# Raw activations for block 1's input projection, the last MLP column by token chunk, and a wide final power in a hybrid conv and state-space layer

## The chip, the cores and the metric

The kernel runs on one core of a Trainium2 chip. The metric is the device time of one execution in microseconds. The core has five engines with queues of their own, which run their instructions in order and wait for each other by semaphores: TensorE (PE, matrix products; PEld is its weight load), VectorE (DVE), ScalarE (ACT), GpSimd (POOL) and SyncE (SP, here the issuer of most transfers). DMA queues move data between HBM and the on-chip memory (SBUF); products land in PSUM.

## The reference

One decoder layer over 2064 tokens (16 meta tokens and 2048 others) with 1024 features:

```python
hn = rms_norm(h, norm_mix_g)
proj = hn @ w_in                          # b_gate, c_gate, v, u: 512 columns each
conv_out = b_gate * causal_dwconv(c_gate * v, conv_w)
ssm_out = s5_group_ssm(u, ...)            # scan over tokens, GELU, half-GLU
mixed = concat([rms_norm(conv_out), rms_norm(ssm_out)])
h = h + mixed @ w_out
hn = rms_norm(h, norm_ffn_g)
up = causal_dwconv(hn @ w_up, ffn_conv_w, ffn_conv_b)   # 2 x 2816 columns, width 3
h = h + (silu(up[..., :2816]) * up[..., 2816:]) @ w_down
y = rms_norm(h, norm_final_g)[:, 16:]
```

`rms_norm` divides each token's vector by its root mean square, so the factor 1/rms is one number for each token; the gain is one number for each feature. Everything is in float32.

## The kernel before

Features lie on the 128 partitions, tokens on the free axis. The tokens are cut into three blocks b = 0, 1, 2 of 688, each into two chunks (quarters q = 2b and 2b+1 of 344 tokens; in block 0 the MLP has 672, two times 336). A float32 product is made of three products of halves: `parts` makes hi (a rounded copy, ScalarE, L248) and lo (the rest, VectorE, L109), and `product` issues hi·hi (L138), hi·lo (L139) and lo·hi (L142).

**Input projection.** `u_block(b)` makes the 512 columns u for the state-space part in four products `pu`, each written from PSUM to `ut` and sent to HBM; `conv_block(b)` makes for j = 0 to 3 the three products `cv`, `cc`, `cb` and from them the convolution: vs from cv, `cvt` = cc·vs, three taps into `tc`, and tc·cb. These products share a PSUM pool of three buffers. The program writes u_block(0), conv_block(0), u_block(2), u_block(1), conv_block(1), conv_block(2), and the steps of the state-space part and the preparation of the next x are put between the products from queues (`prep`, `ssm`). Engines keep the order that a scheduler makes of the program.

x of a quarter can be prepared in two ways. `prep_x` loads it, takes 1/rms of its tokens (`inv_rms`) and splits x·gain·(1/rms): four multiplies t_c (L241) and one hi and one lo instruction for each half of the features. `raw_x` splits x·gain alone, four hi (L393) and four lo (L394) instructions for each half, and takes 1/rms beside it into `rs_of[b]`; since 1/rms is one factor for each token, it is then multiplied in behind the products. Before the change block 0's x and the x for u_block(2) are made by `raw_x`, and all others by `prep_x`. A third argument, `late`, puts the split of a quarter into a list that a later product takes.

`inv_rms_of` has a chain over four engines: the squares summed over features, six small products `st` (L188) with ones so that the sums stand on 115 partitions by 3 columns, mean and epsilon `sv` (VectorE, L198), the power −0.5 `sr` (GpSimd, L199), three diagonals `dg` (L203), one product `sb` (L208) that spreads them to 128 partitions by 344 tokens, and a copy `rs` (ScalarE, L213).

**MLP.** The up projection of one f (128 gate and 128 value columns) goes by seven products of a two-by-two scheme (b11, t4, t1, t2, b22, b21, t3) into z_0 and z_1 (gate and value, both chunks of tokens). `activate` then makes the convolution (ScalarE L1449, two multiply-adds on VectorE L115), silu, the product of gate and value, and its parts `ah`, `al`. 22 f go in chunks of 4, 4, 4, 3, 3 and 4, and after each chunk `down` adds its part of the down projection: `dn` products over the chunk's f, added to HBM by GpSimd's DMA. The products over a pair of output tiles take the last f of the chunk at the end. Under the last chunk of block b the next block's operands (v_b, h_t, l_t and others of `prep_mlp`) are made. The last chunk of block 2 goes by token chunks c, its rows stay in SBUF (`acc`), their squares are summed into `tail_sum` and `tq`, and `finish_last` takes the final 1/rms and multiplies the eight rows.

Of the kernel before, what the change touches and what calls it, by code (L numbers as in the profile page):

```python
# [11 lines left out]
F32 = mybir.dt.float32  # L12
# [5 lines left out]
P = 128  # L18
# [39 lines left out]
def layer_kernel(ctx, tc, xq, pk, w_in, w_glu, w_out, w_up, w_down, ssm_s, ssm_m, y):  # L58
# [317 lines left out]
    rs_of = {}  # L376

    def raw_x(q, res, b, other=False, late=None):
# [30 lines left out]
        yield from inv_rms(xs, QL, f"c{q}", rs_of[b][:, q % 2, :])  # L409

# [479 lines left out]
    def u_block(b, hs, last=False):  # L890
        rhs = rhs_of(hs)
        for m in range(4):
            if last and m == 3:
                while len(late) < 2:
                    prep.step()
            ps = unit(rhs, f"pu_{b}_{m}", m == 0 or last and m == 3)
            ut = cvp.tile([P, NJ, 86], F32, tag="ut", bufs=2, name=f"ut_{b}_{m}")
            if last and m == 3:
                take_late(2)
            by_j = lambda a: a.rearrange("p c (x j) -> p c x j", j=NJ)  # L900
            out = ut.rearrange("p j (c x) -> p c x j", c=2)
            if b in rs_of:
                mul(out, by_j(ps[:, :, :QL]), by_j(rs_of[b]))
            else:
                S.activation(out, by_j(ps[:, :, :QL]), AF.Copy)
            dma(out=u_d[:, m, :, b * 86 : b * 86 + 86].rearrange("j p c -> p j c"), in_=ut)
            after_unit(n_prep=5 if last else 1)

    def conv_block(b, hs, late_after=False, n_prep=1):
        rhs = rhs_of(hs)  # L910

        for j in range(4):
            pv_ = unit(rhs, f"cv_{b}_{j}", False)
            vs = cvp.tile([P, B2], F32, tag="cs", bufs=3, name=f"vs_{b}_{j}")
            if b == 0:
                mul(two(vs), pv_[:, :, :QL], rs_of[0])
# [6 lines left out]
            if b == 0:  # L923
                mul(two(vs), two(vs), rs_of[0])
# [6 lines left out]
            if b == 0:  # L931
                mul(two(tp), two(tp), rs_of[0])
# [69 lines left out]
    prep.add(prep_x(2, hc[1]), prep_x(3, hc[1], other=True, late=late))  # L1002
# [408 lines left out]
    def finish_last(rows, c, terms):  # L1411

        s0, n = y_at(2, c)
        rs = yield from inv_rms_of(terms, D, n, f"last{c}", keep=True)
        for m0, m1 in ((0, 1), (1, 2), (2, 4), (4, 6), (6, 8)):
            for m in range(m0, m1):
                mul(rows(m, c), rows(m, c), rs)
# [13 lines left out]
    for b in range(3):  # L1431
# [16 lines left out]
        def conv(z, t, a):  # L1448
            S.activation(a, z[:, nz - no :], AF.Identity, scale=tap(2, t), bias=col(C_FB + t))  # L1449
# [4 lines left out]
            axpy(a, z[:, nz - no - 1 : nz - 1], tap(1, t), a)  # L1454
            axpy(a, z[:, nz - no - 2 : nz - 2], tap(0, t), a)
# [18 lines left out]
        def up(f, end=False):  # L1474
# [27 lines left out]
            later.append(activate(f, (g, v)))  # L1502
# [3 lines left out]
            tt(v2, X.unsqueeze(1).to_broadcast([P, 2, n]), v2, ALU.add)  # L1506
# [9 lines left out]
        def down(ci, ms, cs=(0, 1), into=None):  # L1516
# [16 lines left out]
            for ks in (range(nk - 1), range(nk - 1, nk)) if len(ms) > 1 else (range(nk),):  # L1533
                for m, ps, w in todo:
# [154 lines left out]
```

## Time and profile before

| | |
|---|---|
| three timed runs | 2183.53, 2181.94, 2178.26 us |
| median | 2181.94 us |
| the profiled execution's own time | 2178.72 us |
| its span in the trace | 2177.0 us |
| mean granted TensorE clock | 0.987 |
| PE busy | 2112.7 us, 97% |
| VectorE, ScalarE, GpSimd busy | 1671.2, 1089.1 and 153.6 us |

The trace holds one execution. Its span leaves 1.7 us of the execution's time outside. A timeline row has the start, the duration, the engine, the line of the kernel, the operation, output and inputs by name, the shape, and in brackets the idle time of that engine before it and what ended it; a row with xN stands for N instructions in a row.

### The profile page before, as it was taken

Reading aid. Unit: us, or ns where it says so; the run is one execution under the profiler, and the core shown is the slowest. Engines: PE = TensorE matmul, PEld = TensorE weight load, DVE = VectorE, ACT = ScalarE, POOL = GpSimd, SP = SyncE. Lnnn points to the kernel's source line nnn. Section 1 sums busy time; section 2 is a strip of 40 time slices with the busy share of each in tenths; the row PEclk is TensorE's granted clock in tenths of the full one; section 3 lists DMA queues with packets and bytes.
Section 4 is the critical chain, followed back from the end, with each engine's and each line's share of the span. In section 5 each row is a group of like instructions: output and inputs, shape, how many; then the busy total and the mean of one; then the engine's idle time right before and its main releaser. Section 6 shows DMA issues by size and latency. Waiting matters only on the chain. (4 is left out here: it accounts for less than half of the span.)

```text
span 2177.0 us, 33169 instructions
## 1 busy us (share of the span) xinstructions
PE 2112.7 (97%) x13012; PEld 2053.0 (94%) x13012; DVE 1671.2 (77%) x2539; ACT 1089.1 (50%) x1659; POOL 153.6 (7%) x174
## 2 busy tenths in 40 slices
PE   8998999999899999999999999999999999999997
PEld 7997999999899999999999999999999999999996
DVE  8788498866857887786669878777868968757776
ACT  4144334236423465555556556555556546545555
POOL 0000000000000000100111010110011010010000
PEclk9898999999999999999999999999999999999998
DMA  7377544352566245725554363744555272564463
GB/s 236 108 210 192 147 142 146 118 162 84 185 223 200 83 109 134 185 70 122 128 135 107 110 157 92 186 111 142 129 131 130 89 191 77 142 133 101 93 173 107
DMA packets 170750, 300.29 MB, mean 138 GB/s; under 512 B 32416, under 2 KB 104800, under 8 KB 170464
## 3 DMA queue, kind: packets, MB, share of 16 engines
q1 hardware_dynamic: 149856, 246.41, 36.8%
q0 software_dynamic: 19584, 47.52, 13.1%
q10 hardware_dynamic: 1152, 4.23, 0.5%
q8 instruction: 102, 1.67, 0.3%
q14 instruction: 56, 0.46, 0.1%
HBM read 214.29 MB, written 83.82 MB: 137 GB/s over the span
## 5 line engine op out<-in xcount | busy, mean ns | idle before, releaser
L109 DVE TENSOR_TENSOR wl_up<-wr_up,wh_up 128x1024 fp32r<-128x1024 f32 x198 | 242.0, 1222 | 137.6 <-ACT wh_up L248 134.9
L138 PE MATMUL dn<-ah,wh_dn 128*128 128x344 f32 (+1 forms) x1024 | 327.7, 324 | 10.2 <-ACT ah L248 8.9
L139 PE MATMUL dn<-al,wh_dn 128*128 128x344 f32 (+1 forms) x1024 | 326.0, 321 | 0.2
L248 ACT ACTIVATE wh_up<-wr_up 128x1024 fp32r<-128x1024 f32 x198 | 210.0, 1061 | 226.8 <-PE dn L139 59.8
L1444 PE MATMUL xy<-h_t,wh_up 128*128 128x344 f32 (+1 forms) x792 | 262.3, 331 | 0.8 <-DVE z L109 0.8
L1446 PE MATMUL xy<-h_t,wl_up 128*128 128x344 f32 (+1 forms) x792 | 252.9, 319 | 0.0
L1445 PE MATMUL xy<-l_t,wh_up 128*128 128x344 f32 (+1 forms) x792 | 252.3, 319 | 0.0
L142 PE MATMUL dn<-ah,wl_dn 128*128 128x344 f32 (+1 forms) x1024 | 248.6, 321 | 0.0
L138 PEld LDWEIGHTS dn<-ah,wh_dn 128*128 128x128 f32 x1024 | 193.7, 190 | 14.6 <-ACT ah L248 9.7
L1546 POOL DMA_DIRECT2D h_d<-ev x136 | 118.3, 870 | 1256.0 <-ACT ev L1542 1242.5
L139 PEld LDWEIGHTS dn<-al,wh_dn 128*128 128x128 f32 x1024 | 194.9, 190 | 2.0 <-DVE al L109 1.2
L1444 PE MATMUL xy<-h_b,wh_up 128*128 128x344 f32 (+1 forms) x528 | 175.2, 333 | 4.7 <-ACT ev L1542 1.9
L142 PEld LDWEIGHTS dn<-ah,wl_dn 128*128 128x128 f32 x1024 | 178.6, 190 | 0.0
L1445 PE MATMUL xy<-l_b,wh_up 128*128 128x344 f32 (+1 forms) x528 | 168.5, 319 | 0.0
L1446 PE MATMUL xy<-h_b,wl_up 128*128 128x344 f32 (+1 forms) x528 | 167.1, 319 | 0.0
L1444 PEld LDWEIGHTS xy<-h_t,wh_up 128*128 128x128 f32 x792 | 148.9, 188 | 18.3 <-ACT z L1489 11.4
L248 ACT ACTIVATE wh_dn<-wr_dn 128x512 fp32r<-128x512 f32 (+1 forms) x144 | 85.7, 595 | 134.7 <-issue 56.3
L1445 PEld LDWEIGHTS xy<-l_t,wh_up 128*128 128x128 f32 x792 | 149.5, 189 | 0.0
L1446 PEld LDWEIGHTS xy<-h_t,wl_up 128*128 128x128 f32 x792 | 149.3, 188 | 0.0
L115 DVE SCALAR_TENSOR_TENSOR g<-z,pv,g 128x688 f32<-128x688 f32 (+1 forms) x132 | 122.3, 927 | 24.0 <-ACT g L1449 23.2
L115 DVE SCALAR_TENSOR_TENSOR v<-z,pneg,v 128x688 f32<-128x688 f32 (+1 forms) x132 | 122.5, 928 | 10.3 <-ACT v L1449 9.0
L109 DVE TENSOR_TENSOR wl_dn<-wr_dn,wh_dn 128x512 fp32r<-128x512 f32 (+1 forms) x144 | 92.4, 645 | 46.0 <-ACT wh_dn L248 45.2
(413 smaller groups left out, 5326.2 us busy)
## 6 DMA issues: line engine op xcount, KB each, us to landing
wr_up<-in_w_up SPq DMA_DIRECT2D x132, 512.0 KB, 5.5
h_d<-ev POOLq DMA_DIRECT2D x88, 344.0 KB, 6.8
wr_dn<-in_w_down SPq DMA_DIRECT2D x96, 256.0 KB, 2.6
wr_cw<-in_w_in SPq DMA_DIRECT2D x36, 512.0 KB, 4.5
h_d<-ev POOLq DMA_DIRECT2D x48, 336.0 KB, 6.8
x_c<-in_xq SPq DMA_DIRECT2D x16, 688.0 KB, 4.6
wr_dn<-in_w_down SPq DMA_DIRECT2D x48, 192.0 KB, 2.3
xr<-in_xq SPq DMA_DIRECT2D x24, 344.0 KB, 3.8
```

Source lines behind the costliest of these rows:

```text
L109: V.tensor_tensor(out, a, b, op=op)
L115: V.scalar_tensor_tensor(out=out, in0=a, scalar=s, in1=b, op0=ALU.mult, op1=ALU.add)
L138: T.matmul(ps[c], hi[:, k, :], xh, start=k == 0, stop=False)
L139: T.matmul(ps[c], hi[:, k, :], xl, start=False, stop=False)
L142: T.matmul(ps[c], lo[:, k, :], xh, start=False, stop=k == nk - 1)
L248: S.activation(hi, t, AF.Copy)
L1444: T.matmul(ps, hi[:, j, :], xh[:, j, :], start=start and j == 0, stop=False, **kw)
L1445: T.matmul(ps, hi[:, j, :], xl[:, j, :], start=False, stop=False, **kw)
L1446: T.matmul(ps, lo[:, j, :], xh[:, j, :], start=False, stop=j == 3, **kw)
L1546: G.dma_start(out=h_d[:, m, s0 : s0 + no], in_=ev, accum_op=ALU.add)
```

## The change

The diff has three parts, in three places of the program.

**A. Block 1's x.** Quarters 2 and 3 go by `raw_x`. So `u_block(1)` reads PSUM with a VectorE multiply by `rs_of[1]` and not with a ScalarE copy, after both quarters' 1/rms are there (`rs_done`), and `conv_block(1)` has the three multiplies for each j that `conv_block(0)` has: vs from PSUM times rs (in place of a ScalarE copy), vs times rs again, tc times rs.

**B. The last f of the last chunk of every block.** `activate_halves` goes through the convolution, silu, product and split by token chunk; the value's last addition is in two halves; and the first pair of `down` tiles of the last chunk takes its last f chunk by chunk. The copies of the halo (`context`) now stand ahead of the first tap in all `activate`s.

**C. The end.** For the last token chunk `finish_last` sums squares with a 128-wide matrix of ones, two products of 344 columns, so that every partition has every token's sum; mean and epsilon (128x344) on VectorE, the power (128x344) on GpSimd, no diagonal and no broadcast; rows 3 and 6 of the eight are multiplied on GpSimd, the others on VectorE.

```diff
--- before.py
+++ after.py
@@ -373,7 +373,7 @@
     def rs_tile(name):
         return cp.tile([P, 2, QM], F32, tag="rsk", bufs=1, name=name)
 
-    rs_of = {}
+    rs_of, rs_done = {}, {}
 
     def raw_x(q, res, b, other=False, late=None):
 
@@ -407,6 +407,7 @@
         if b not in rs_of:
             rs_of[b] = rs_tile(f"rs_{b}")[:, :, :QL]
         yield from inv_rms(xs, QL, f"c{q}", rs_of[b][:, q % 2, :])
+        rs_done[b] = rs_done.get(b, 0) + 1
 
 
     sgn = col(C_SGN)
@@ -900,6 +901,8 @@
             by_j = lambda a: a.rearrange("p c (x j) -> p c x j", j=NJ)
             out = ut.rearrange("p j (c x) -> p c x j", c=2)
             if b in rs_of:
+                while rs_done.get(b, 0) < 2:
+                    prep.step()
                 mul(out, by_j(ps[:, :, :QL]), by_j(rs_of[b]))
             else:
                 S.activation(out, by_j(ps[:, :, :QL]), AF.Copy)
@@ -912,24 +915,24 @@
         for j in range(4):
             pv_ = unit(rhs, f"cv_{b}_{j}", False)
             vs = cvp.tile([P, B2], F32, tag="cs", bufs=3, name=f"vs_{b}_{j}")
-            if b == 0:
-                mul(two(vs), pv_[:, :, :QL], rs_of[0])
+            if b < 2:
+                mul(two(vs), pv_[:, :, :QL], rs_of[b])
             else:
                 S.activation(two(vs), pv_[:, :, :QL], AF.Copy)
             after_unit(n_prep=n_prep)
             pc = unit(rhs, f"cc_{b}_{j}", False)
             cv = cvp.tile([P, B2 + 2], F32, tag="cvt", bufs=1, name=f"cvt_{b}_{j}")
             V.tensor_copy(cv[:, 0:2], halo[:, j, :])
-            if b == 0:
-                mul(two(vs), two(vs), rs_of[0])
+            if b < 2:
+                mul(two(vs), two(vs), rs_of[b])
             tt(two(cv[:, 2:]), pc[:, :, :QL], two(vs), ALU.mult)
             V.tensor_copy(halo[:, j, :], cv[:, B2 : B2 + 2])
             tp = cvp.tile([P, B2], F32, tag="cs", bufs=3, name=f"tc_{b}_{j}")
             S.activation(tp, cv[:, 2:], AF.Copy, scale=col(C_CW + 8 + j))
             axpy(tp, cv[:, 1 : B2 + 1], col(C_CW + 4 + j), tp)
             axpy(tp, cv[:, 0:B2], col(C_CW + j), tp)
-            if b == 0:
-                mul(two(tp), two(tp), rs_of[0])
+            if b < 2:
+                mul(two(tp), two(tp), rs_of[b])
             after_unit(n_prep=n_prep)
             if late_after and j == 3:
                 while len(late) < 2:
@@ -999,7 +1002,7 @@
     next(ahead[0])
     conv_block(0, hc[0], late_after=True, n_prep=4)
 
-    prep.add(prep_x(2, hc[1]), prep_x(3, hc[1], other=True, late=late))
+    prep.add(raw_x(2, hc[1], 1), raw_x(3, hc[1], 1, other=True, late=late))
     u_block(2, hu, last=True)
     until(hc[1], 2)
     prep.add(prep_x(4, hc[2]), prep_x(5, hc[2], late=late))
@@ -1411,10 +1414,20 @@
     def finish_last(rows, c, terms):
 
         s0, n = y_at(2, c)
-        rs = yield from inv_rms_of(terms, D, n, f"last{c}", keep=True)
+        if c == 0:
+            rs = yield from inv_rms_of(terms, D, n, f"last{c}", keep=True)
+        else:
+
+            ps = aux_tile("st_last")[:, :n]
+            for i, a in enumerate(terms):
+                T.matmul(ps, ones, a, start=i == 0, stop=i == len(terms) - 1)
+            v, rs = z_tile("v_last")[:, :n], z_tile("r_last")[:, :n]
+            V.tensor_scalar(v, ps, 1.0 / D, EPS, op0=ALU.mult, op1=ALU.add)
+            G.tensor_tensor(rs, v, mhalf[:, 0:1].to_broadcast([P, n]), op=ALU.pow)
         for m0, m1 in ((0, 1), (1, 2), (2, 4), (4, 6), (6, 8)):
             for m in range(m0, m1):
-                mul(rows(m, c), rows(m, c), rs)
+                eng = G if c and m in (3, 6) else V
+                eng.tensor_tensor(rows(m, c), rows(m, c), rs, op=ALU.mult)
             for m in range(m0, m1, 2):
                 mm = min(2, m1 - m)
                 a = acc[m // 2].rearrange("p (m c) t -> p c m t", c=2)[:, c, m % 2 : m % 2 + mm, :n]
@@ -1445,14 +1458,42 @@
                 T.matmul(ps, hi[:, j, :], xl[:, j, :], start=False, stop=False, **kw)
                 T.matmul(ps, lo[:, j, :], xh[:, j, :], start=False, stop=j == 3, **kw)
 
-        def conv(z, t, a):
-            S.activation(a, z[:, nz - no :], AF.Identity, scale=tap(2, t), bias=col(C_FB + t))
+        def context(z, t):
+
             if b:
                 S.activation(z[:, :o], halo[:, t, :], AF.Copy)
             if b < 2:
                 S.activation(halo[:, t, :], z[:, nz - 2 :], AF.Copy)
-            axpy(a, z[:, nz - no - 1 : nz - 1], tap(1, t), a)
-            axpy(a, z[:, nz - no - 2 : nz - 2], tap(0, t), a)
+
+        def conv_of(z, t, a, i, n):
+
+            i0 = nz - no + i
+            a = a[:, i : i + n]
+            S.activation(a, z[:, i0 : i0 + n], AF.Identity, scale=tap(2, t), bias=col(C_FB + t))
+            axpy(a, z[:, i0 - 1 : i0 - 1 + n], tap(1, t), a)
+            axpy(a, z[:, i0 - 2 : i0 - 2 + n], tap(0, t), a)
+
+        def conv(z, t, a):
+            context(z, t)
+            conv_of(z, t, a, 0, no)
+
+        def activate_halves(f, zs):
+
+            v, g = (fp.tile([P, MAX_OUT], F32, tag="g", bufs=3, name=f"{c}_{b}_{f}")[:, :no] for c in "vg")
+            hi, lo = (fp.tile([P, MAX_OUT], F32R, tag="act", bufs=10, name=f"a{c}_{b}_{f}")[:, :no] for c in "hl")
+            context(zs[0], f)
+            for c in range(2):
+                conv_of(zs[0], f, g, c * nn, nn)
+                h = g[:, c * nn : (c + 1) * nn]
+                S.activation(h, h, AF.Silu)
+            yield
+            context(zs[1], FT + f)
+            act[f] = (hi, lo)
+            for c in range(2):
+                conv_of(zs[1], FT + f, v, c * nn, nn)
+                r = slice(c * nn, (c + 1) * nn)
+                mul(v[:, r], g[:, r], v[:, r])
+                parts(v[:, r], hi[:, r], lo[:, r])
 
         def activate(f, zs):
 
@@ -1499,11 +1540,15 @@
             form(z1, w, 1, "b21")
             tt(g2[:, 0, :], z1, g2[:, 0, :], ALU.add)
             work()
-            later.append(activate(f, (g, v)))
+            later.append((activate_halves if end else activate)(f, (g, v)))
             form(X, w, 0, "t3", start=False)
             if end:
                 work()
-            tt(v2, X.unsqueeze(1).to_broadcast([P, 2, n]), v2, ALU.add)
+            if end:
+                for c in range(2):
+                    tt(v2[:, c, :], X, v2[:, c, :], ALU.add)
+            else:
+                tt(v2, X.unsqueeze(1).to_broadcast([P, 2, n]), v2, ALU.add)
             feed.done()
             mark[0] = g[:, o : o + 1]
             if f < f0_last:
@@ -1531,6 +1576,11 @@
                 return tuple(a[:, cs[i] * nn : (cs[i] + 1) * nn] for a in act[f0 + k])
 
             for ks in (range(nk - 1), range(nk - 1, nk)) if len(ms) > 1 else (range(nk),):
+                if len(ms) > 1 and ks[0] == nk - 1 and ci == last:
+                    for i in range(len(cs)):
+                        for m, ps, w in todo:
+                            product([ps[i]], w, lambda k, _: rhs_down(k, i), nk, ks=ks)
+                    continue
                 for m, ps, w in todo:
                     product(ps, w, rhs_down, nk, ks=ks)
             for m, ps, _ in todo:
```

How the instructions move at the three places follows as the engines' queues have them, the numbers at the end of names being serial numbers of tiles. First VectorE ahead of u_block(1): before, from the last squares of the second quarter (sq_c) to its split;

```order
L109 TENSOR_TENSOR sq_c_0_2030<-sq_c_0_2030,sq_c_1_2032 128x4x344
L109 TENSOR_TENSOR ut_3_2118<-pu_3_2063,rs_1437 128x86x8
L109 TENSOR_TENSOR sq_c_0_2030<-sq_c_0_2030 128x2x344
L109 TENSOR_TENSOR wl_u_2193<-wr_u_1977,wh_u_2192 128x1024
L109 TENSOR_TENSOR sq_c_0_2030<-sq_c_0_2030 128x344
L198 TENSOR_SCALAR sv_c_2041<-st_c_2037 115x3
L203 TENSOR_SCALAR dg_c_2045<-ident,sr_c_2042 115x115 x3
L241 SCALAR_TENSOR_TENSOR t_c_0_2053<-x_c_0_1968,pv,rs_c_2051 128x344 x4
L241 SCALAR_TENSOR_TENSOR t_c_1_2058<-x_c_1_1970,pv,rs_c_2051 128x344 x4
L109 TENSOR_TENSOR l_c_0_2120<-t_c_0_2053,h_c_0_2119 128x4x344
```

and now:

```order
L109 TENSOR_TENSOR sq_c_0_2032<-sq_c_0_2032 128x344
L394 SCALAR_TENSOR_TENSOR l_c_0_2096<-x_c_0_1970,pv,h_c_0_2095 128x344 x4
L394 SCALAR_TENSOR_TENSOR l_c_1_2106<-x_c_0_2030,pv,h_c_1_2105 128x344 x4
L109 TENSOR_TENSOR ut_3_2094<-pu_3_2039,rs_1437 128x86x8
L198 TENSOR_SCALAR sv_c_2121<-st_c_2117 115x3
L109 TENSOR_TENSOR wl_u_2196<-wr_u_1977,wh_u_2195 128x1024
L203 TENSOR_SCALAR dg_c_2125<-ident,sr_c_2122 115x115 x2
L109 TENSOR_TENSOR wi_2585<-tab_coarse,tab_fine 128x544
L203 TENSOR_SCALAR dg_c_2125<-ident,sr_c_2122 115x115
```

The t_c and the wide l_c are gone, the split by lo (L394, from x and hi alone) stands ahead of sv_c, and sv_c and the diagonals dg_c stand behind eight l_c, ut and a weight's lo part. On PE, in the same place, before:

```order
L139 MATMUL pu_2_2249<-l_c_0_1956,wh_u_2130 128x344
L188 MATMUL st_c_2037<-ones,sq_c_0_2030 115x1 x3
L208 MATMUL sb_c_2049<-dg_c_2045,ones 128x344
L138 MATMUL pu_0_2129<-h_c_0_2119,wh_u_1973 128x344
L138 MATMUL pu_1_2191<-h_c_0_2119,wh_u_2064 128x344
L138 MATMUL pu_2_2249<-h_c_0_2119,wh_u_2130 128x344
```

and now:

```order
L142 MATMUL pu_3_2039<-h_c_1_1795,wl_u_1899 128x344
L188 MATMUL st_c_2117<-ones,sq_c_0_2032 115x1 x3
L138 MATMUL pu_0_2132<-h_c_0_1869,wh_u_1973 128x344
L139 MATMUL pu_0_2132<-l_c_0_1870,wh_u_1973 128x344
L142 MATMUL pu_0_2132<-h_c_1_1879,wl_u_1974 128x344
L208 MATMUL sb_c_2129<-dg_c_2125,ones 128x344
L138 MATMUL pu_0_2132<-h_c_0_2095,wh_u_1973 128x344
```

Before, u_block(1) had products of its first quarter (h_c_0_1955 and others) ahead of st and sb and those of the second behind them; now pu_0 has its 24 products of the first quarter between st and sb (rows 4 and 5 are the first and the last shown), and those of the second quarter behind sb.

Second, VectorE at the last f (21) of block 1, before:

```order
L115 SCALAR_TENSOR_TENSOR g_21_15985<-z_21_0_15853,pv,g_21_15985 128x688
L109 TENSOR_TENSOR wl_dn_5_3_15994<-wr_dn_5_3_15888,wh_dn_5_3_15993 128x512
L115 SCALAR_TENSOR_TENSOR v_21_15984<-z_21_1_15854,pneg,v_21_15984 128x688
L109 TENSOR_TENSOR l_t_2_16119<-v_b_2_15390,h_t_2_16118 128x4x344
L115 SCALAR_TENSOR_TENSOR v_21_15984<-z_21_1_15854,pneg,v_21_15984 128x688
L1190 SCALAR_TENSOR_TENSOR v_b_2_15390<-v_b_2_15390,v_b_2_15392 128x4x344
L109 TENSOR_TENSOR v_21_15984<-g_21_15985,v_21_15984 128x688
L109 TENSOR_TENSOR l_t_2_16279<-v_b_2_15391,h_t_2_16278 128x4x344
```

and now:

```order
L115 SCALAR_TENSOR_TENSOR g_21_16007<-z_21_0_15875,pv,g_21_16007 128x344 x4
L109 TENSOR_TENSOR z_21_1_15876<-xy_21_15877,z_21_1_15876 128x344 x2
L109 TENSOR_TENSOR wl_dn_5_3_16023<-wr_dn_5_3_15910,wh_dn_5_3_16022 128x512
L115 SCALAR_TENSOR_TENSOR v_21_16006<-z_21_1_15876,pneg,v_21_16006 128x344 x4
L109 TENSOR_TENSOR v_21_16006<-g_21_16007,v_21_16006 128x344 x2
L1193 SCALAR_TENSOR_TENSOR v_b_2_15412<-v_b_2_15412,v_b_2_15414 128x4x344
L109 TENSOR_TENSOR al_21_16009<-v_21_16006,ah_21_16008 128x344 x2
```

The multiply v<-g,v stood behind l_t and a step of v_b, and now its halves stand ahead of v_b, as do the last taps. Third, VectorE behind the last product of the program, before:

```order
L109 TENSOR_TENSOR acc_20684<-dn_5_7_1_21050,acc_20684 128x344
L198 TENSOR_SCALAR sv_last_21074<-st_last_21067 115x3
L203 TENSOR_SCALAR dg_last_21078<-ident,sr_last_21075 115x115 x3
L109 TENSOR_TENSOR acc_20675<-acc_20675,sb_last_21082 128x344 x2
L109 TENSOR_TENSOR acc_20678<-acc_20678,sb_last_21082 128x344 x2
L109 TENSOR_TENSOR acc_20681<-acc_20681,sb_last_21082 128x344 x2
L109 TENSOR_TENSOR acc_20684<-acc_20684,sb_last_21082 128x344 x2
```

now, with GpSimd's last rows behind VectorE's:

```order
L109 TENSOR_TENSOR acc_20728<-dn_5_7_1_21094,acc_20728 128x344
L1425 TENSOR_SCALAR v_last<-st_last 128x344
L1430 TENSOR_TENSOR acc_20719<-acc_20719,r_last 128x344 x2
L1430 TENSOR_TENSOR acc_20722<-acc_20722,r_last 128x344
L1430 TENSOR_TENSOR acc_20725<-acc_20725,r_last 128x344 x2
L1430 TENSOR_TENSOR acc_20728<-acc_20728,r_last 128x344
L1426 TENSOR_TENSOR r_last<-v_last,mhalf 128x344
L1430 TENSOR_TENSOR acc_20722<-acc_20722,r_last 128x344
L1430 TENSOR_TENSOR acc_20728<-acc_20728,r_last 128x344
```

The last three rows are GpSimd's. sv_last, dg_last and sb_last are gone; v_last goes to GpSimd's power, whose result r_last both engines multiply.

## The prediction

> **What bounds the kernel now.** I read the page first, for the engine that has no slack:
>
> ```profile
> PE 2112.7 (97%) x13012; PEld 2053.0 (94%) x13012; DVE 1671.2 (77%) x2539; ACT 1089.1 (50%) x1659; POOL 153.6 (7%) x174
> ```
>
> TensorE is busy for 97% of the span, so no engine can be relieved for a gain: the change does not take one large product away, and what it can win are places where PE stands still, the half clock that follows them, and the tail after the last product. Next I read the windows (us, then busy time and instructions of PE, PEld, DVE, ACT, POOL, the granted clock, DMA share, GB/s) around the places of the diff.
>
> ```profile
> 200.00:210.00 10.00, 3.09 (x7) 1.59 (x7) 6.76 (x14) 3.48 (x4) 0.85 (x1) 0.53 0.55 133
> 220.00:230.00 10.00, 10.00 (x65) 10.00 (x64) 1.23 (x1) 2.86 (x3) 0.00 (x0) 1.00 0.69 147
> 260.00:270.00 10.00, 10.00 (x63) 9.80 (x62) 10.00 (x16) 2.88 (x3) 0.00 (x0) 1.00 0.29 92
> 200.60:214.25 13.65, 7.29 (x21) 5.84 (x22) 9.39 (x15) 5.88 (x5) 0.64 (x1) 0.50 0.48 136
> 1176.80:1180.21 3.41, 3.30 (x13) 3.27 (x13) 3.41 (x4) 2.21 (x5) 0.44 (x1) 0.51 0.00 0
> 1658.10:1661.51 3.41, 3.34 (x12) 3.34 (x13) 3.41 (x4) 2.15 (x5) 0.46 (x1) 0.50 0.00 0
> ```
>
> PE is idle for 7 of the 10 us from 200 on, and then works at clock 0.50 until 214.25. The two short windows are the same behind the last up products of blocks 0 and 1: PE is busy again, but at half clock for 3.41 us, which costs 1.7 us each. Rows two and three show VectorE idle behind the first place (1.23 of 10 us) and full 40 us later.
>
> **Part A, block 1's x.** Now the timeline of PE (start, duration, in brackets the idle time and its releaser):
>
> ```profile
> 197.82 0.32 PE L139 MATMUL pu<-l_c,wh_u 128*128 128x344 f32 x1
> 199.28 0.76 PE L188 MATMUL st_c<-ones,sq_c 128*115 128x1 f32 x6 [1.15 <-DVE sq_c L109]
> 202.11 1.51 PE L208 MATMUL sb_c<-dg_c,ones 115*128 115x344 f32 x2 [2.07 <-DVE dg_c L203]
> 207.63 1.23 PE L138 MATMUL pu<-h_c,wh_u 128*128 128x344 f32 x3 [4.01 <-ACT h_c L248]
> ```
>
> From 197.82 to 207.63, 9.8 us, PE does only the sums of squares (0.76) and the broadcast (1.51) of 1/rms of one x quarter, and waits. The other engines in that time:
>
> ```profile
> 198.73 0.50 DVE L109 TENSOR_TENSOR sq_c<-sq_c 128x344 f32<-128x344 f32 x1
> 203.66 0.46 ACT L213 ACTIVATE rs_c<-sb_c 128x344 f32<-128x344 f32 x1 [9.00 <-PE sb_c L208]
> 204.16 3.99 DVE L241 SCALAR_TENSOR_TENSOR t_c<-x_c,pv,rs_c 128x344 f32<-128x344 f32 x8 [2.10 <-ACT rs_c L213]
> 206.23 1.35 ACT L248 ACTIVATE h_c<-t_c 128x1376 fp32r<-128x1376 f32 x1 [2.11 <-DVE t_c L241]
> ```
>
> The chain is squares, sums, power, diagonal, broadcast, copy, then x·gain·rs, and only then the hi part for which PE waits. The change splits x·gain at once: t_c goes, and h_c and l_c need nothing but x. PE then waits no longer for this chain ahead of its first product. It meets it one place later: in the new order the broadcast stands on PE behind the first 24 products of u_block(1), and its diagonal behind eight l_c, the ut multiply and the power. Rolling the engines forward in the new order with the durations above, PE stands before that broadcast for about 2 us. Saved: 9.8 − 0.7 (the sums and the broadcast, still to be done, at full clock) − 2 = 7.1 us. With a stall that short I take the window at half clock to go too: from 207.63 to 214.25 PE worked 6.6 us for 3.3 us of work. Together 10.4 us.
>
> What A adds is on VectorE. By kinds:
>
> ```profile
> L394 DVE SCALAR_TENSOR_TENSOR l_c<-x_c,pv,h_c 128x344 fp32r<-128x344 f32 x16 | 8.5, 581 | 0.0
> L109 DVE TENSOR_TENSOR ut<-pu,rs 128x688 f32<-128x688 f32 x4 | 5.9, 1464 | 0.0
> L109 DVE TENSOR_TENSOR tc<-tc,rs 128x688 f32<-128x688 f32 x3 | 2.6, 871 | 0.0
> PE cb L138 <- DVE cvt L109: 0.8, 1, 0.8
> ```
>
> (The first three are of block 0's x and of the convolution of block 0 and the u of block 2, where the forms are in use already; the last is a row of the waits between 270 and 330 us: who waits for whom, us, times, longest.) Sixteen l_c of 0.58 replace as many t_c of like price and four 1376-wide subtractions: no cost. Four ut multiplies of 1.46 move from ScalarE to VectorE: 5.9 us where VectorE has 1.2 of 10 us to do, so hidden; without that room it is 5.9 us at most. The twelve new 688-wide multiplies of conv_block(1) are the other matter. They are 12 × 0.87 = 10.4 us, by starts 0.78 apart 9.4, in a stretch whose VectorE is full. There cb_j is held by cvt_j, since the three PSUM buffers are taken; the row shows 0.8 us of it already. Two of the three multiplies of each j come ahead of cvt_j. Bounds: 0, if they only push back the SSM's tables, and 9.4. Rolling forward, the second and third cvt come 1.0 and 1.4 us later: 2.4 us, taken. **A: 10.4 − 2.4 = 8.0 us gained**, from 1.0 to 10.4.
>
> **Part B, the last f of each block.** For block 1, in time, on VectorE, ScalarE and PE:
>
> ```profile
> 1652.61 0.93 DVE L115 SCALAR_TENSOR_TENSOR v<-z,pneg,v 128x688 f32<-128x688 f32 x1
> 1653.45 1.59 DVE L1190 SCALAR_TENSOR_TENSOR v_b<-v_b,v_b 128x1376 f32<-128x1376 f32 x1
> 1654.96 0.87 DVE L109 TENSOR_TENSOR v<-g,v 128x688 f32<-128x688 f32 x1
> 1656.33 0.76 ACT L248 ACTIVATE ah<-v 128x688 fp32r<-128x688 f32 x1
> 1657.14 0.90 PE L138 MATMUL dn<-ah,wh_dn 128*128 128x344 f32 x4 [2.61 <-ACT ah L248]
> ```
>
> PE waits 2.61 us for ah. VectorE has a step of the next block's preparation, v_b, between the convolution and the multiply, and ScalarE its h_t before ah. In the new order the halves of v and their multiply stand ahead of v_b, so that the first ah half is due near 1652.9, before PE asks for it at 1654.4; the al halves are ready within 0.8 us after that. I take 2.3 of the 2.61 us, and the 1.7 of the half clock behind: 4.0 us. In block 0 and block 2:
>
> ```profile
> 1175.94 0.88 PE L138 MATMUL dn<-ah,wh_dn 128*128 128x336 f32 x4 [2.88 <-ACT ah L248]
> 2125.50 1.90 DVE L115 SCALAR_TENSOR_TENSOR v<-z,pneg,v 128x688 f32<-128x688 f32 x2
> 2127.51 0.88 DVE L109 TENSOR_TENSOR v<-g,v 128x688 f32<-128x688 f32 x1
> 2128.41 0.78 ACT L248 ACTIVATE ah<-v 128x688 fp32r<-128x688 f32 x1 [2.54 <-DVE v L109]
> 2129.24 0.94 PE L138 MATMUL dn<-ah,wh_dn 128*128 128x344 f32 x2 [3.37 <-ACT ah L248]
> ```
>
> In block 0 v_b stays ahead of the halves, so a half multiply, not the order, is won: about 1 us of the 2.88, and half of the 1.7 at half clock, 1.9. In block 2 the chain axpy, axpy, multiply, hi has no other work in it; in halves, the first hi ends after about four steps of 0.5 and one of 0.45, some 0.9 us earlier than 2129.19. The 2.5 us left of the stall is long enough to keep the half clock. **B: 1.9 + 4.0 + 0.9 = 6.8 us**, from 3 (no clock, half of the stalls) to 11 (all three stalls and all the clock). [...]
>
> [...]
>
> **Part C, the tail.** The broadcast of the first chunk, and then what follows the last product, in order:
>
> ```profile
> 2153.88 0.74 PE L208 MATMUL sb_last<-dg_last,ones 115*128 115x344 f32 x2
> 2164.79 0.36 PE L188 MATMUL st_last<-ones,tq 128*115 128x1 f32 x2 [0.90 <-ACT tq L1599]
> 2166.30 0.85 POOL L199 TENSOR_TENSOR sr_last<-sv_last,mhalf 115x3 f32<-115x3 f32 x1 [16.82 <-DVE sv_last L198]
> 2168.02 1.52 PE L208 MATMUL sb_last<-dg_last,ones 115*128 115x344 f32 x2 [2.07 <-DVE dg_last L203]
> 2169.57 3.47 DVE L109 TENSOR_TENSOR acc<-acc,sb_last 128x344 f32<-128x344 f32 x8 [1.61 <-PE sb_last L208]
> ```
>
> From 2164.79 to the last multiply at 2173.04 are 8.25 us. After the change: one product of 344 columns, 0.8 (the broadcast of the first chunk, at full clock, took 0.74); v from PSUM, 0.5 (one 344-wide VectorE step); three crossings of 0.1; a power over 128x344 of time X; then six multiplies at the present pitch of 0.43, 2.6 us, against two on POOL beside them. That is 4.2 + X, so the tail changes by X − 4.05. X decides, and no power of that width is in the trace. What POOL shows (the start of the kernel):
>
> ```profile
> 20.52 2.23 POOL L199 TENSOR_TENSOR sr_c<-sv_c,mhalf 115x3 f32<-115x3 f32 x1 [19.20 <-DVE sv_c L198]
> masks.py:199 POOL TENSOR_SCALAR_AFFINE_SELECT ident<-ident 128x128 f32<-128x128 f32 x1 | 0.3, 293 | 0.1
> ```
>
> Lower bound: all 0.85 of the narrow power is entry and a column costs as in the select, 0.293 / 128 = 2.3 ns: 0.85 + 0.8 = 1.6 us. Upper: all of it goes by column, 0.85 / 3 × 344 = 97 us. The same three columns take from 0.85 to 2.23 us, so most of it is not the columns; I take X = 8, under the geometric middle of the two ends (12), nearer the select. The two POOL multiplies I put at 1.2 each, between the select's pace (0.8) and the 1.3 at which they would outlast VectorE. **C: a loss of 4.0 us**, from a gain of 2.4 to a loss of 93.
>
> [...]
>
> **The sum.** 8.0 + 6.8 − 4.0 = 10.8 us. The profiled execution took 2178.72, which gives 2167.9; it lies 3.2 under the median of the three runs, 2181.94, which gives 2171.1. I say 2169.
>
> **The rivals.** First, on the other side: **the power goes by columns**. At 40 ns a column X is 13.8 us and leaves a gain of 5; from X = 19 (55 ns) the whole gain of 14.8 is gone, at 100 ns X is 34 and the time 2196, at the upper bound 2259. For it: the narrow power takes three times the select's time with 3 columns to its 128. Against: the spread of the same three columns. Second, **VectorE binds in conv_block(1)**: all 9.4 us of the new multiplies arrive at PE. For it: the full window at 260; against: only one wait of 0.8 us there now, and table work that can fall behind. A is 1.0, the time 2176. Third, **a cheap power**, X about 2: the tail gains 2 us rather than losing 4, time 2163. Fourth, **the clock doesn't come back**: shorter stalls still bring the half clock, so A loses 3.3 and B 2.6 of their sums, time 2175. For it: the 2.61 us stall that did.
>
> **How the numbers follow.** A measurement of this kernel tells 0.3%, 6.5 us, from no change. Forecast 0.42 (faster 0.36, same 0.06); power by columns 0.24 (same 0.04, slower 0.20); VectorE bound 0.12 (0.06 and 0.06); cheap power 0.14 (faster); clock 0.08 (0.04 and 0.04). Faster 0.60, same 0.20, slower 0.20. Range: down to 2156, where all gains are whole and the power is cheap; up to 2195, a power of 34 us. Beyond lie some 0.05 below and 0.14 above. The forecast's own range is 2162 to 2176.
>
> **What would show it.** A: no PE idle time over 2.5 us from 190 to 210, full clock there, and waits of cb for cvt of 2 to 3 us between 250 and 320. B: the [2.61] of dn on ah gone in block 1, 1 us less in blocks 0 and 2. C: one POOL row of 128x344, 8 us long, between v_last and the multiplies, with DVE waiting for it. Wrong would be: a power over 19 us, stalls in conv_block(1) of over 8 us, or a stall elsewhere in the stages that took up what was won.

## The result: slower by 35 us, with one power of 55 us at the end

The changed kernel takes 2214.96 us (median of four runs, 2213.08 to 2215.20), the kernel before 2180.10 in the same comparison: a ratio of 1.0157, 95% interval 1.0141 to 1.0173. The prediction said 2169, with a range of 2156 to 2195. The profiled execution of the change took 2215.2 us with a span of 2213.4.

The page of the changed kernel gives it away in two lines, the busy times and the row of POOL over 40 slices of the span (each digit a share in tenths):

```profile
PE 2106.4 (95%) x13002; PEld 2046.9 (92%) x13002; DVE 1680.8 (76%) x2567; ACT 1086.1 (49%) x1675; POOL 210.7 (10%) x176
...
POOL 0000000000000010110001001011100101100118
```

PE works 6 us less than before in a span 36 us longer, and POOL, at 153.6 before, has 57 us more, in the last slices. The timeline there, of the changed kernel (start, duration, then the row):

```profile
2147.04 0.31 PE L142 MATMUL dn<-ah,wl_dn_7b 128*128 128x344 f32 x1
2148.48 0.85 PE L1423 MATMUL st_last<-tq,ones 128*128 128x344 f32 x2 [0.43 <-ACT tq L1649]
2149.36 0.52 DVE L1425 TENSOR_SCALAR v_last<-st_last 128x344 f32<-128x344 f32 x1 [1.46 <-PE st_last L1423]
2150.03 55.17 POOL L1426 TENSOR_TENSOR r_last<-v_last,mhalf 128x344 f32<-128x344 f32 x1 [16.90 <-DVE v_last L1425]
2205.23 3.85 DVE L1430 TENSOR_TENSOR acc<-acc,r_last 128x344 f32<-128x344 f32 x6 [55.34 <-POOL r_last L1426]
2205.27 2.15 POOL L1430 TENSOR_TENSOR acc<-acc,r_last 128x344 f32<-128x344 f32 x2
```

The power takes 55.17 us, and VectorE waits 55.34 for it. From the start of the last down product to the end of the span are 66.4 us (2213.4 − 2147.04); before they were 13.7:

```profile
2163.34 0.32 PE L142 MATMUL dn<-ah,wl_dn_7b 128*128 128x344 f32 x1
```

So the end costs 52.7 us more, and the last product starts 16.3 us earlier. How the 16.3 build up, by a product that stands in the same place in both: first the last cb of block 1, then the last product ahead of the stall at each block's end. Before:

```profile
367.73 0.42 PE L138 MATMUL cb<-h_c,wh_cw 128*128 128x344 f32 x1 [1.27 <-DVE cvt L109]
1172.59 0.47 PE L142 MATMUL dn<-ah,wl_dn 128*128 128x336 f32 x2
1654.06 0.48 PE L142 MATMUL dn<-ah,wl_dn 128*128 128x344 f32 x2
2125.56 0.32 PE L142 MATMUL dn<-ah,wl_dn 128*128 128x344 f32 x1
```

After:

```profile
358.27 0.42 PE L138 MATMUL cb<-h_c,wh_cw 128*128 128x344 f32 x1 [0.96 <-DVE cvt L109]
1163.22 0.47 PE L142 MATMUL dn<-ah,wl_dn 128*128 128x336 f32 x2
1644.24 0.48 PE L142 MATMUL dn<-ah,wl_dn 128*128 128x344 f32 x2
2112.20 0.32 PE L142 MATMUL dn<-ah,wl_dn 128*128 128x344 f32 x1
```

The leads are 9.5, 9.4, 9.8 and 13.4 us, and 16.3 at the last product. Part A gave 9.4. Part B gave 0.4 from the end of block 0 to that of block 1, 3.6 in the next stage and 2.9 in the last: 6.9.

Each trace is one execution, and the steps of part B are good to some 3 us only. Run c, below, is the kernel before with part C alone, so up to its last sums it is the same program; yet in its trace the five products start at 367.67, 1173.31, 1657.61, 2128.69 and 2166.64: 0.1 earlier than in the kernel before, and then 0.7, 3.6, 3.1 and 3.3 us later. The timed executions of one program differ in the same way: 18 of the kernel before go from 2173.39 us, at a mean granted clock of 0.989, to 2185.37 at 0.984.

Part A in the timeline and the window of the change, where PE before had 9.5 us with only the sums and the broadcast to do:

```profile
197.72 0.32 PE L142 MATMUL pu<-h_c,wl_u 128*128 128x344 f32 x1
198.90 0.82 PE L208 MATMUL sb_c<-dg_c,ones 115*128 115x344 f32 x2 [0.85 <-DVE dg_c L203]
199.29 0.58 PE L138 MATMUL pu<-h_c,wh_u 128*128 128x344 f32 x1
...
200.00:210.00 10.00, 10.00 (x66) 10.00 (x65) 7.18 (x9) 1.60 (x3) 0.00 (x0) 1.00 0.70 178
```

One stall of 0.85 us is left, and the clock is 1.00 from 200 to 210, where it was 0.53. The stalls and clocks of part B in the change:

```profile
1164.64 0.42 PE L138 MATMUL dn<-ah,wh_dn 128*128 128x336 f32 x1 [0.94 <-ACT ah L248]
1166.26 0.42 PE L138 MATMUL dn<-ah,wh_dn 128*128 128x336 f32 x1 [0.89 <-ACT ah L248]
1523.48 0.42 PE L138 MATMUL dn<-ah,wh_dn 128*128 128x344 f32 x1 [1.83 <-ACT ev L1592]
1645.72 0.42 PE L139 MATMUL dn<-al,wh_dn 128*128 128x344 f32 x1 [0.38 <-DVE al L109]
2114.33 0.42 PE L138 MATMUL dn<-ah,wh_dn 128*128 128x344 f32 x1 [1.81 <-ACT ah L248]
...
1163.00:1173.00 10.00, 7.76 (x47) 6.90 (x46) 10.00 (x13) 7.23 (x13) 2.60 (x3) 1.00 0.22 28
1524.40:1527.81 3.41, 3.41 (x14) 3.41 (x14) 3.41 (x8) 0.47 (x2) 1.05 (x2) 0.51 1.08 292
1644.00:1654.00 10.00, 9.22 (x57) 8.65 (x56) 9.95 (x10) 7.76 (x11) 2.60 (x3) 1.00 0.39 78
2114.90:2118.31 3.41, 3.38 (x12) 2.93 (x12) 2.50 (x5) 2.51 (x5) 0.00 (x0) 0.51 0.09 15
```

The stalls of 2.88, 2.61 and 3.37 us became 0.94 with 0.89, 0.38, and 1.81. In this trace the clock stays full behind the first two places; behind the third it is half for 3.41 us, where it had been for 6.83:

```profile
2129.20:2136.03 6.83, 6.75 (x21) 5.90 (x22) 3.50 (x7) 3.48 (x7) 0.00 (x0) 0.50 0.25 78
```

A half-clock window of 3.41 us that the trace before does not have lies at 1524.40, with PE busy; at clock 0.51 it costs 1.7 us, half of its length, and this is the larger part of what block 0's end had won. It follows a stall of 1.83 us on ev (ScalarE's copy of a dn product out of PSUM) inside block 1, near the start of its last chunk. Neither can be put down to the change. The kernel before has a stall of 1.85 us near there, with nothing slow behind it (clock 1.00 from 1537 to 1545), and run c, the same program up to there, has one of 4.34 with half clock behind it. Before, then run c:

```profile
1539.43 0.43 PE L1444 MATMUL xy<-h_b,wh_up 128*128 128x344 f32 x1 [1.85 <-ACT ev L1542]
...
1542.35 0.65 PE L1454 MATMUL xy<-h_b,wh_up 128*128 128x344 f32 x1 [4.34 <-ACT ev L1552]
1542.18:1545.60 3.42, 3.25 (x11) 3.25 (x12) 3.42 (x6) 2.22 (x4) 1.73 (x2) 0.50 0.52 27
```

Nor is the full clock at block 0's end sure. A with B ran twice, in runs ab and ab2 below, as one and the same program. The first trace has full clock there; the second has the same two stalls and half clock behind them:

```profile
1167.33 0.73 PE L138 MATMUL dn<-ah,wh_dn 128*128 128x336 f32 x3 [0.95 <-ACT ah L248]
1168.95 0.42 PE L138 MATMUL dn<-ah,wh_dn 128*128 128x336 f32 x1 [0.89 <-ACT ah L248]
1169.74:1173.15 3.41, 3.41 (x14) 3.32 (x14) 3.39 (x3) 1.81 (x4) 0.26 (x1) 0.50 0.00 0
```

What differs is where the stalls lie. Within one trace the half-clock windows start whole multiples of 3.413 us apart: in the kernel before at 88.00, 200.63, 548.79, 1176.85, 1658.12, 2129.16 and 2166.71, which are 33, 102, 184, 141, 138 and 11 such steps; in the changed kernel at 87.43, 541.40, 582.37, 1524.44, 2114.95 and 2152.50, which are 133, 12, 276, 173 and 11. The steps that lie between are an estimate, this grid carried on from a measured start. In ab2 both stalls lie in the one grid window ahead of 1169.74: 1.84 us of standing still. In the changed kernel the grid has an edge at 1166.04, inside the second stall, which leaves 1.61 us in one window and 0.22 in the next. Its stall of 1.83 us lies whole in the window from 1521.03 to 1524.44; the 1.85 us of the kernel before are cut at 1538.65 into 1.07 and 0.78. In these four the half clock follows where PE stood still for 1.8 us of a grid window, and not where it did for 1.6 or less.

### The profile page after: what moved, and what is told of

Same layout as the page of the kernel before. It is cut to its first block, busy times and chain, and to the rows that moved or that the text cites. A ratio compares the mean times of both kernels' runs of the same rounds, so it can differ in the third digit from the quotient of the medians.

```text
span 2213.4 us, 33233 instructions
## 1 busy us (share of the span) xinstructions
PE 2106.4 (95%) x13002; PEld 2046.9 (92%) x13002; DVE 1680.8 (76%) x2567; ACT 1086.1 (49%) x1675; POOL 210.7 (10%) x176
## 4 chain that ended last, share of the span: by engine, by line
PE 69%; DVE 4%; POOL 2%; ACT 1%; DMA 1%; issue 1%; DVEq 0%; ACTq 0%; POOLq 0%; SPq 0%
PE xy L1457 10%; PE xy L1459 9%; PE xy L1458 9%; PE dn L138 7%; PE dn L139 7%; PE dn L142 7%; PE pz L1459 4%; PE pz L1458 4%; PE pz L1457 4%; POOL r_last L1426 2%; PE po L138 2%; PE po L142 2%; PE po L139 2%; ACT h_ms L1058 1%; PE pg L138 1%
## 5 line engine op out<-in xcount | busy, mean ns | idle before, releaser
L115 DVE SCALAR_TENSOR_TENSOR g<-z,pv,g 128x688 f32<-128x688 f32 (+3 forms) x138 | 123.0, 896 | 25.3 <-ACT g L1472 24.0
L115 DVE SCALAR_TENSOR_TENSOR v<-z,pneg,v 128x688 f32<-128x688 f32 (+3 forms) x138 | 122.9, 896 | 8.3 <-ACT v L1472 7.0
## 6 DMA issues: line engine op xcount, KB each, us to landing
x_c<-in_xq SPq DMA_DIRECT2D x16, 688.0 KB, 6.0
```

The lines of the kernel that those rows point to most:

```text
L115: V.scalar_tensor_tensor(out=out, in0=a, scalar=s, in1=b, op0=ALU.mult, op1=ALU.add)
```

## The experiments

**Each part alone, and A with B.** Theory 1 is that the wide power is the whole loss and A and B gain; the rivals are that the gains depend on each other or on where half-clock windows fall, and that the 55 us belong to that execution. A and B together leave the end as it was:

```diff
-        if c == 0:
-            rs = yield from inv_rms_of(terms, D, n, f"last{c}", keep=True)
-        else:
...
+        rs = yield from inv_rms_of(terms, D, n, f"last{c}", keep=True)
-                eng = G if c and m in (3, 6) else V
-                eng.tensor_tensor(rows(m, c), rows(m, c), rs, op=ALU.mult)
+                mul(rows(m, c), rows(m, c), rs)
```

> Parts A and B with the end as before (narrow power, diagonal, broadcast, all eight rows on VectorE). Theory 1 (the whole loss is the wide power, A and B each gain): in the changed kernel the last product ended 16.3 us earlier than before (2147.2 for 2163.5), so 16 us faster than before, about 2164. Theory 2 (the wide end itself, with its wide sums and split rows, moved the last product's end too, or A and B gain only because of where the half-clock windows happened to fall): between 5 and 12 us faster, 2168 to 2175.

Measured: 2162.56 us against 2179.25, ratio 0.9924 (0.9905 to 0.9944), 16.6 us faster. Part C alone is the same lines the other way round, on the kernel before.

> Part C alone. Theory 1: the time from the last product to the end of the span was 13.5 us before and 66.2 in the changed kernel, so 52.7 us slower than before, about 2233, with one power of 55 us on GpSimd. Theory 2 (the 55 us belong to this one execution, or to values or neighbours of the changed kernel): the power takes another time, below 45 us, and the kernel is under 2223.

Measured: 2234.03 us, ratio 1.0250 (1.0230 to 1.0270), 54.8 us slower. Its power, with neither A nor B in the program:

```profile
2169.63 55.17 POOL L1423 TENSOR_TENSOR r_last<-v_last,mhalf 128x344 f32<-128x344 f32 x1 [16.86 <-DVE v_last L1422]
```

The same 55.17. Then part A alone (`raw_x` for quarters 2 and 3 and the multiplies that follow from it, nothing else of the diff) and part B alone (the halves of the last f, nothing else):

> Part A alone. Theory 1: 9.4 us faster, as the rows of block 1's convolution came that much earlier in the changed kernel: about 2171. Theory 2 (the saving is given back later, at the stalls that B takes away, because products that come earlier wait longer there): 0 to 4 us faster, 2176 to 2180.

> Part B alone. Theory 1: the three ends of the up products gave 2.4, 3.8 and 2.3 us in the changed kernel, so some 8 us faster, about 2172, each stall of dn on ah shorter and no half clock behind it. Theory 2 (most of it was half-clock windows that fell elsewhere by the new phase): 2 to 4 us faster, 2176 to 2178, with half-clock windows at other places.

Measured: A 2172.64 us, ratio 0.9965 (0.9951 to 0.9979), by it 7.6 us faster; B 2172.68 us, ratio 0.9972 (0.9959 to 0.9985), by it 6.1 us faster. For A this leaves theory 2 out. B lies halfway between its two theories, and its interval holds numbers of both. The sum is 13.7 for 16.6 together; the intervals (4.6 to 10.7, 3.3 to 8.9, 12 to 21) do not tell these apart. The profile of A alone has something that theory 1 left out, a longer wait for the same ev inside block 1, and half clock behind it:

```profile
1531.56 0.65 PE L1447 MATMUL xy<-h_b,wh_up 128*128 128x344 f32 x1 [4.61 <-ACT ev L1545]
...
1529.10:1535.90 6.80, 4.34 (x15) 4.35 (x16) 6.80 (x12) 4.29 (x7) 1.73 (x2) 0.50 0.41 56
```

The kernel before waits 1.85 us there, in the row of 1539.43 above, but run c, without A, waits 4.34, so the long wait is not A's doing; what makes it long in some executions was not tested. The profile of B alone has full clock at the ends of blocks 0 and 1, half clock for 3.41 us at that of block 2, and two half-clock windows that the trace before lacks, from 688.0 and 742.6, as theory 2 of B expected. Since such windows come and go between executions of one program, one trace does not show that B moved them.

**What a power costs.** On A with B, behind the end of the program and with nothing beside them, GpSimd runs powers of other sizes (`pv` holds the last 1/rms, `pc` the constant 2.0):

```diff
+        if c == 1:
...
+            for np_, w in ((P, 3), (P, 3), (P, 8), (P, 32), (P, 86), (P, 172), (64, 172), (16, 172), (16, 3), (115, 3)):
+                G.tensor_tensor(pr[:np_, :w], pv[:np_, :w], mhalf[:np_, 0:1].to_broadcast([np_, w]), op=ALU.pow)
+            G.tensor_tensor(pr[:, :172], pc[:, :172], mhalf[:, 0:1].to_broadcast([P, 172]), op=ALU.pow)
+            G.tensor_tensor(pr, pv, pc, op=ALU.mult)
+            G.tensor_tensor(pr, pv, pc, op=ALU.mult)
```

> Parts A and B as in the kernel before that one, and behind the end, with nothing beside them, powers of other sizes on GpSimd: 128x3 twice, 128x8, 128x32, 128x86, 128x172, 64x172, 16x172, 16x3, 115x3, 128x172 of the constant 2.0, and two multiplies of 128x344. Theory 1 (the power costs by column, whatever the partitions, beside an entry): 0.16 us a column from 55.17 / 344, so 128x172 27.6 us, 128x86 13.9, 128x32 5.3, 64x172 and 16x172 the same 27.6. Theory 2 (by element): 64x172 13.8, 16x172 3.5. Theory 3 (by value): the constant takes another time than the data. The multiplies: theory 1 of the end says 0.9 us each without VectorE beside them, against 1.07 in the changed kernel.

Measured, eight of the twelve groups of POOL by shape in that stretch (line, engine, operation, names, shapes, count, busy us, mean ns, idle time before):

```profile
L1431 POOL TENSOR_TENSOR probe_r<-probe_c,mhalf 128x172 f32<-128x172 f32 x1 | 27.8, 27781 | 0.1
L1430 POOL TENSOR_TENSOR probe_r<-probe_v,mhalf 128x172 f32<-128x172 f32 x1 | 27.8, 27767 | 0.1
L1430 POOL TENSOR_TENSOR probe_r<-probe_v,mhalf 16x172 f32<-16x172 f32 x1 | 27.8, 27756 | 0.1
L1430 POOL TENSOR_TENSOR probe_r<-probe_v,mhalf 128x86 f32<-128x86 f32 x1 | 14.1, 14051 | 0.1
L1430 POOL TENSOR_TENSOR probe_r<-probe_v,mhalf 128x32 f32<-128x32 f32 x1 | 5.4, 5413 | 0.1
L1430 POOL TENSOR_TENSOR probe_r<-probe_v,mhalf 128x3 f32<-128x3 f32 x2 | 1.7, 848 | 6.5 <-ACT probe_v L1427 6.5
L1432 POOL TENSOR_TENSOR probe_r<-probe_v,probe_c 128x344 f32<-128x344 f32 x1 | 0.9, 907 | 0.1
L1430 POOL TENSOR_TENSOR probe_r<-probe_v,mhalf 16x3 f32<-16x3 f32 x1 | 0.8, 840 | 0.1
```

Theory 1 holds, theories 2 and 3 fall. From 3 to 172 columns the time grows by 26.92 us, 0.159 us a column; the entry is 0.848 − 3 × 0.159 = 0.37 us; and 0.37 + 344 × 0.159 = 55.2, the 55.17 of the change. The sizes between fit: 128x32 would be 5.5 by this and took 5.41. Sixteen partitions cost as much as 128, and a constant as much as data.

**Rows on two engines.** The changed kernel with its power, all eight rows on VectorE:

```diff
-                eng = G if c and m in (3, 6) else V
-                eng.tensor_tensor(rows(m, c), rows(m, c), rs, op=ALU.mult)
+                mul(rows(m, c), rows(m, c), rs)
```

> The changed kernel with all eight rows multiplied on VectorE. Theory 1 (the two engines hold each other up at reads from SBUF, so the split is worth nothing): the eight take 3.5 us against 3.85 for six beside GpSimd's two, the time within 1 us of the changed kernel's 2215. Theory 2 (the split saves two of eight rows): 1 us slower, the eight taking 5.1 us at the pace of 0.64 seen there.

Measured: 2214.56 us, 0.4 below the changed kernel's 2214.96, with ratios to before of 1.0171 (1.0156 to 1.0186) and 1.0157 (1.0141 to 1.0173): times cannot tell 1 us here, so the rows decide:

```profile
2204.02 3.50 DVE L109 TENSOR_TENSOR acc<-acc,r_last 128x344 f32<-128x344 f32 x8 [55.34 <-POOL r_last L1426]
```

Eight rows take 3.50 us alone and six took 3.85 beside GpSimd's two: 0.44 against 0.64 each. GpSimd's multiply took 1.07 beside VectorE and 0.91 alone, by the last experiment. The split is worth nothing, as theory 1 had it; its reads from SBUF were a guess, and no run shows where the two hold each other up.

**The multiplies of block 1's convolution.** A with B, without the twelve multiplies by 1/rms there:

```diff
-            if b < 2:
+            if b == 0:
                 mul(two(vs), pv_[:, :, :QL], rs_of[b])
 ...
-            if b < 2:
+            if b == 0:
                 mul(two(vs), two(vs), rs_of[b])
 ...
-            if b < 2:
+            if b == 0:
                 mul(two(tp), two(tp), rs_of[b])
```

> Parts A and B without the twelve multiplies by 1/rms in the convolution of block 1 (a ScalarE copy takes vs from PSUM again; the convolution of block 1 lacks the factor). Theory 1 (they cost what block 1 lost between the start of its convolution and its end, 11.2 to 9.5): 1.7 us faster than A and B, about 2161. Theory 2 (they are hidden by tables that fall behind): the same as A and B, 2162.5. Theory 3 (they bind): 6 to 9 us faster, about 2155.

Measured: 2159.30 us, ratio to before 0.9926 (0.9907 to 0.9945). By medians it is 3.3 us under A with B, by ratios 0.2 over it, so the times do not settle theories 1 and 2. In the profiles PE waits for cvt, in the stretch from 250 to 370 us, first of A with B, then without the multiplies, then of the kernel before:

```profile
PE cb L138 <- DVE cvt L109: 3.0, 3, 1.0
```

```profile
PE cb L138 <- DVE cvt L109: 2.0, 2, 1.3
```

```profile
PE cb L138 <- DVE cvt L109: 2.1, 2, 1.3
```

One wait of three goes, 1.0 us, and with it one of 0.3 us for tc. That is far from the 6 to 9 us of theory 3.

**Another way to the same 1/rms.** If only the power is wrong in part C, a wide end with another step should gain. On the changed kernel, with all rows on VectorE, a square root on ScalarE and a reciprocal on VectorE:

```diff
-            V.tensor_scalar(v, ps, 1.0 / D, EPS, op0=ALU.mult, op1=ALU.add)
-            G.tensor_tensor(rs, v, mhalf[:, 0:1].to_broadcast([P, n]), op=ALU.pow)
+            S.activation(v, ps, AF.Sqrt, scale=1.0 / D, bias=eps_c)
+            V.reciprocal(rs, v)
...
+            S.activation(warm, ones[:, 0:1], AF.Sqrt)
```

> The changed kernel with the power replaced: a square root of the summed squares on ScalarE, straight from PSUM, its table loaded ahead of the last products, then a reciprocal on VectorE, and all eight rows on VectorE. Theory 1 (only the power made the wide end slow): from the last product's end 0.9 + 0.5 + 0.6 + 3.5 against the 8.3 of the narrow chain, so 2 to 3 us faster than A and B alone, about 2160, and 55 faster than the changed kernel. Theory 2 (a reciprocal of 344 columns or the table load stands in the path): no faster than A and B, 2162 to 2166.

Measured: 2165.45 us, ratio 0.9947 (0.9932 to 0.9962): 50 us under the changed kernel, and no faster than A with B. Theory 2: the table came in the path although a first use of the square root stood ahead (the scheduler had put that at 2.0 us, at the program's beginning, with other tables behind it), and the reciprocal takes 2.30 us:

```profile
2150.00 1.28 ACT L1428 ACT_TABLE_LOAD   x1
2151.29 0.55 ACT L1428 ACTIVATE v_last<-st_last,eps_c 128x344 f32<-128x344 f32 x1
...
2151.87 2.30 DVE L1429 RECIPROCAL r_last<-v_last 128x344 f32<-128x344 f32 x1 [3.03 <-ACT v_last L1428]
```

So a last attempt, a logarithm and an exponential, with the table loaded behind the last f, beside A with B once more:

```diff
+            S.activation(v, ps, AF.Ln, scale=1.0 / D, bias=eps_c)
+            S.activation(rs, v, AF.Exp, scale=-0.5)
...
+                S.activation(warm, v[:, 0:1], AF.Ln, scale=0.0, bias=ones[:, 0:1])
```

> The changed kernel with the power replaced by two steps of ScalarE, a logarithm of the summed squares straight from PSUM and an exponential of -0.5 times it, the table loaded behind the last f's product, and all eight rows on VectorE. Theory 1 (the wide sums are worth their place as soon as the power's step is short): from the last sum on 0.55 + 0.5 + 3.5 against 7.4 for the narrow chain, 2 to 3 us faster than A and B with the narrow end, about 2160. Theory 2 (the narrow chain's steps are no longer than a wide chain's, as with the square root): the same time as A and B within 1 us.

> Parts A and B with the end as before, once more beside the kernel with the logarithm. Theory 1 and 2 alike: 16.5 us faster than before, ratio 0.992 to 0.993.

Measured: 2161.52 us, ratio 0.9913 (0.9897 to 0.9928), for the logarithm; 2164.54, ratio 0.9923 (0.9908 to 0.9937), for A with B. The intervals overlap, so the times show no gain over the narrow chain; both kernels are faster than the kernel before and the changed one. The traces say a little more. From the start of the last down product to the first multiplied row the logarithm's end takes 4.70 us (2149.76 to 2154.46); the narrow end takes 6.23 in run ab (2145.97 to 2152.20) and 5.55 in ab2 (2150.67 to 2156.22), where its broadcast took 0.85 us (1.52 at half clock in the kernel before). So the wide end is 0.9 to 1.5 us shorter there, between the two theories. With the square root it is 6.24. The exponential had a table of its own in the path, where 0.5 us had been put down:

```profile
2152.08 0.55 ACT L1428 ACTIVATE v_last<-st_last,eps_c 128x344 f32<-128x344 f32 x1 [0.32 <-PE st_last L1426]
2152.65 1.28 ACT L1429 ACT_TABLE_LOAD   x1
2153.94 0.49 ACT L1429 ACTIVATE r_last<-v_last 128x344 f32<-128x344 f32 x1
2154.46 3.50 DVE L112 TENSOR_TENSOR acc<-acc,r_last 128x344 f32<-128x344 f32 x8 [3.84 <-ACT r_last L1429]
```

## Why the prediction was wrong

**The step that failed is the price of the power, X = 8 us; it is 55.17.** With that one number the prediction's sum, 2178.72 − 14.8 + (55.17 − 4.05), is 2215.0; measured 2214.96. That it fits so well is luck: A and B gave 16.3 in the traces and not 14.8, and the end lost 52.7 and not 51.1, and the two misses cancel.

The mechanism is the first rival, "the power goes by columns", at 160 ns a column; the prediction gave it 0.24 and let the range end at a power of 34 us. The argument for a small X was that the same three columns take from 0.85 to 2.23 us, so that most of the 0.85 is not the columns. It doesn't follow: the lowest time bounds entry and columns together, and a spread above it, whatever makes it, says nothing about how the 0.85 divides. It divides into 0.37 and 0.48. The other row, the select at 2.3 ns a column, is of another operation, and 70 times too cheap. The upper end, 97 us, came from the operation itself, and should have had more weight. A row of 3 columns cannot price one of 344, and the honest forecast was a wide one: if each doubling between 1.6 and 97 us counts alike, a power over 25 us, which makes the kernel slower by more than the 6.5 us that the prediction could tell, has a chance of about a third.

**Part A**, put at 8.0, gave 9.4. At the first product of conv_block(1) the lead was 11.2 us (237.3 to 226.1), where the saved stall and clock were put at 10.4; 0.85 us of stall is left where 2 was forecast. The sum had read the place a little wrongly: its 9.8 us begin with the last product, 0.32, and it left out a third stall there, 0.84 us for l_c at 209.70. The convolution then took back 1.7 us, where 2.4 was forecast; 1.2 of it are waits of PE, those for cvt from 2.1 to 3.0 and a new one of 0.3 for tc. (The prediction's 0.8 for the kernel before was of a stretch that ended at 330, ahead of the last cb.) That VectorE binds there, the second rival, is out.

**Part B**, put at 6.8, gave 6.9 in the traces, by other terms, so the agreement is luck here too; B alone gave 6.1, with an interval of 3.3 to 8.9. Block 0: 0.4 for 1.9. The stall of 2.88 fell by 1.05, as the forecast of 1 had it, and the clock came back whole, but 1.7 went in the half-clock window at 1524.40, which no step had, and some 0.6 elsewhere. Block 1: 3.6 for 4.0. Block 2: 2.9 for 0.9, since the stall fell by 1.6 and not 0.9, and the half clock behind it lasted 3.41 us and not 6.83. That 2 us of stall would let the clock come back, and 2.5 us not, was the author's estimate; here 1.81 us had half clock behind it. The fourth rival (the clock doesn't come back) fell at A's place and at the end of block 1; at the end of block 0 the clock came back in the changed kernel and in run ab, and not in ab2, so there it depends on the execution.

**Part C** apart from X: the wide sum 0.85 for 0.8, v 0.52 for 0.5, GpSimd's multiplies 1.07 each for 1.2, and the three crossings, 0.1 each by the author's estimate, 0.03, 0.15 and 0.03; the six multiplies took 3.85 for 2.6, for the pitch of VectorE alone was used for VectorE beside GpSimd. That is 1.25 of the 1.6 us that the end lost beyond the sum. The third rival, a cheap power, is out.

## What to carry to other kernels

A price read from a tiny instance splits into entry and slope only by a second size; where the trace has one size, the wide end of the bound is a case of its own, with a chance of its own, and no middle stands in for it. Spreading work over all partitions to save a broadcast multiplies an operation's columns (here 3 to 344), so it pays only for steps that are cheap by the column; the narrow chain with its diagonal and product took 4.8 us from its last sums to the first row (2164.79 to 2169.57), the wide power alone 55. Giving a second engine a share of an elementwise step is worth measuring: here eight rows on one engine took less time (3.50 us) than six beside two (3.85). Last, before gains of a few us are read from one trace each, compare two traces of one program: here they differ by 3.3 us at the last product.

## What the runs showed of the hardware

GpSimd's power (f32, exponent −0.5, nothing beside it, run probe) took 0.848 us for 3 columns and 27.77 for 172, on 16 partitions 0.840 and 27.76: 0.37 us and 0.159 us a column. A reciprocal of 128x344 on VectorE took 2.30 us (run sqrt), where the multiply and add of v_last over that size took 0.52. A logarithm followed by an exponential had a table load of 1.28 us between them (run lnexp). Stalls of 0.95 and 0.89 us close together had a half-clock window of 3.41 us behind them in run ab2, and stalls of 0.94 and 0.89 none in the changed kernel; one of 1.83 us had such a window in the changed kernel, and one of 1.85 had none in the kernel before. So the length of a stall alone does not decide. In these four places PE stood still within one window of the 3.41 us grid, with PE's ends as the profile models them, for 1.84 and 1.83 us where half clock followed, and for 1.61 and 1.07 where it did not. The border isn't as clean everywhere: in run b a window with 0.99 us of standing still (from 684.6) has half clock behind it, and in the changed kernel one with 1.81 (from 534.6) has none. No run was made to move a stall on purpose, so what decides was not shown.
